# Seven block products for eight in eleven of the gates' and the output product's slots of a decoder block

## The chip, the core and the metric

One core of one Trainium2 chip runs the whole kernel in one launch. TensorE (PE) does the matrix products into eight PSUM banks, ScalarE (ACT) and VectorE (DVE) do the elementwise work, SyncE (SP) issues the DMAs, GpSimd (POOL) does a handful of small operations. The metric is the time of one execution on the device in microseconds (us), the median of several runs.

## The reference, cut to what matters

One layer over 256 tokens of width 2048, all in float32. The lines below are the part that the change touches: two gates, each a product of the normed input with 2048 columns of `w_in`, scale the two branches' up-projections; their sum goes through `w_out`.

```python
h = rmsnorm(x, attn_norm_w[l])
proj = h @ w_in[l]
rq, rk, rv, rg, mq, mk, mv, g_ret, g_moba = jnp.split(proj, split_at, axis=-1)
...
merged = jax.nn.sigmoid(g_ret) * (o_ret @ w_ret_up[l]) + jax.nn.sigmoid(g_moba) * (o_moba @ w_moba_up[l])
x = x + merged @ w_out[l]
h2 = rmsnorm(x, ffn_norm_w[l])
up = causal_dwconv(h2 @ w_ffn_up[l], conv_w[l], conv_b[l])
a, b = jnp.split(up, 2, axis=-1)
x = x + (jax.nn.silu(a) * b) @ w_ffn_down[l]
return rmsnorm(x, final_norm_w)
```

`o_ret` (1024 wide) and `o_moba` (1024 wide) are the results of a chunked retention and of a block attention, which run beside the earlier products.

## The kernel before

**Products.** Each float32 operand is split into two parts, `hi` (a copy rounded to the matmul's type, on ACT) and `lo` (full minus `hi`, on DVE), and a product is the sum of three: hi·hi, hi·lo and lo·hi. `mm3` issues these three matmuls. A matmul of the stretch in question has a stationary block of 128x128 activations and 512 moving columns of weights, and adds into one PSUM bank (128 x 512 float32).

**Slots.** The weights stream in once, as halves of 128x1024 float32 (512 KB: two 128-row pieces of one 512-column group). Two halves make a slot. The loop at L894 runs over the groups of `plan()`: gates `gr` and `gm` (4 slots each, 512 columns per group `c`), up-projections `um` and `ur` (2 slots each), and this for four columns `c`; then `wo` (4 groups of 4 slots), then `up` and the down product `dn`. In a plain slot PE does 2 halves x 2 pieces x 2 token tiles x 3 = 24 matmuls (`products`, L883 to L891).

**What sets the order.** All order is that of the code. While PE works on slot n, the code issues the parts of slot n+1: `part` (L146) puts the `hi` copies on ACT and the `lo` subtractions on DVE, then issues the load for the half four ahead (L144, `RAW_BUFS` is 4, so the raw tile of slot n+1 is that of slot n-1, and it is free when its `lo` is done). `whi` and `wlo` have four buffers (`PART_BUFS`), so the `hi` copies of slot n+1 wait until PE is through with the same half of slot n-1. Elementwise work between the groups is written as generators (`spawn`), of which each runs one stage per slot (`run_tasks`), after that slot's parts; the PE work that they ask for (`flip`, a transpose) goes into the middle of the slot's matmuls (`issue`, L180).

**Names.** `sr` and `sm` hold the gates' sigmoids and then the merged columns (`keep_sig` L470, `gate_moba` L474, `merge` L477); `ftr` are PSUM tiles for the transposes of a merged column into `mgh` and `mgl`, the two parts of `wo`'s activations (`flipped`, L450); `xp` is the residual input that `closed` (L627) adds to `wo`'s result, and `x2` the sum. `acc` is a pair of PSUM banks.

**Seven for eight.** In the down product only, 12 of 44 slots are of another kind: the 2x2 blocks of a slot (two token tiles, two 128-row pieces, two column groups) are multiplied with seven block products in place of eight, so with 21 matmuls. For this `seven_parts` (L674) forms four sums of the weight blocks on DVE (L686 to L691) besides the parts, `seven_sums` (L708) four sums of the activation blocks once per `k`, and the accumulators take eight PSUM banks: four main ones and four extra ones, `e0` to `e3`, which `gathered` (L762) folds into the outputs after the last such slot of a pair of groups.

## Time and profile before

| | us |
|---|---|
| median of 3 runs | 1432.77 (1432.64 to 1432.97) |
| the profiled execution, whole | 1433.07 |
| its span, first to last instruction | 1431.3 |
| PE busy in the span | 1420.4 |
| DVE busy | 977.1 |
| ACT busy | 743.4 |

The table is read from the top: the whole time of the profiled execution is 1.8 us more than its span, and the span is nearly all PE work. The first gate is read out of PSUM (`sr`) at 367 us, and the four `wo` groups are added to the residual from 631 to 699 us; the first matmul on activations' sums, so the first slot of seven products, stands at 1213 us.

### The profile page before, as it was taken

The page shows a single profiled execution, that of the slowest core. Times are in us where ns is not written, and L with a number is a line of the kernel's source. Part 1 is how long each engine was busy: PE and PEld are TensorE (multiplying, and loading weights), DVE is VectorE, ACT ScalarE, POOL GpSimd, SP SyncE. Part 2 cuts the span into 40 slices and gives each one's busy share as a digit, 9 for nine tenths or more (in the row PEclk, how much of TensorE's full clock was granted, in tenths as well). Part 3 has the DMA queues.
Part 4 walks back from the last instruction along what each step waited for, and adds up shares of the span by engine and source line. Part 5 has one row for each costly group of instructions (what it writes and reads, how often), then busy time and mean ns, then how long its engine had stood idle before and what let it go on. Part 6 is the DMA issues. An engine that isn't in the chain of part 4 may idle for free. (4 is left out here: it accounts for less than half of the span.)

```text
span 1431.3 us, 19149 instructions
## 1 busy us (share of the span) xinstructions
PE 1420.4 (99%) x7290; PEld 1214.8 (85%) x7290; DVE 977.1 (68%) x1296; ACT 743.4 (52%) x1006; POOL 6.0 (0%) x14
## 2 busy tenths in 40 slices
PE   9999999999999999999999999999999999999997
PEld 7888888888888888888888888888888888888886
DVE  6687656657554545455567777777777778898787
ACT  6545454544544444444465555555555555555553
POOL 0000000000000000000000000000000000000000
PEclk9999999999999999999999999999999999999999
DMA  8755565555566666666656666565665655656664
GB/s 295 263 181 163 163 190 167 189 175 189 180 186 196 187 195 186 195 214 200 195 188 189 194 182 197 182 195 188 188 194 181 199 181 168 198 192 206 206 215 167
DMA packets 77836, 276.22 MB, mean 193 GB/s; under 512 B 8720, under 2 KB 10288, under 8 KB 77744
## 3 DMA queue, kind: packets, MB, share of 16 engines
q1 hardware_dynamic: 77312, 274.27, 60.3%
q8 instruction: 57, 0.93, 0.3%
q10 hardware_dynamic: 432, 0.73, 0.1%
q14 instruction: 35, 0.29, 0.1%
HBM read 272.86 MB, written 2.10 MB: 192 GB/s over the span
## 5 line engine op out<-in xcount | busy, mean ns | idle before, releaser
L162 DVE TENSOR_TENSOR wlo<-raw,whi 128x1024 fp32r<-128x1024 f32 (+1 forms) x481 | 573.3, 1219 | 373.9 <-ACT whi L161 239.4
L161 ACT ACTIVATE whi<-raw 128x1024 fp32r<-128x1024 f32 (+1 forms) x481 | 502.2, 1056 | 513.7 <-PE acc L170 372.8
L170 PE MATMUL acc<-xb,whi 128*128 128x512 f32 x1920 | 466.2, 392 | 1.2 <-ACT whi L161 1.2
L170 PEld LDWEIGHTS acc<-xb,whi 128*128 128x128 f32 x1920 | 350.7, 188 | 68.8 <-ACT whi L161 2.3
L170 PE MATMUL acc<-whi,xb 128*128 128x512 f32 x896 | 282.1, 391 | 0.0
L170 PEld LDWEIGHTS acc<-xb,wlo 128*128 128x128 f32 x1920 | 250.8, 191 | 12.3
L170 PE MATMUL acc<-xb,wlo 128*128 128x256 f32 x1920 | 254.6, 282 | 0.0
L170 PEld LDWEIGHTS acc<-whi,xb 128*128 128x128 f32 x896 | 168.3, 188 | 34.4
L170 PE MATMUL acc<-wlo,xb 128*128 128x512 f32 x448 | 174.6, 390 | 0.0
L170 PEld LDWEIGHTS acc<-wlo,xb 128*128 128x128 f32 x448 | 84.2, 188 | 16.7
L170 PE MATMUL acc<-wlo,gh 128*128 128x512 f32 x224 | 87.4, 390 | 0.2 <-DVE wlo L162 0.2
L170 PE MATMUL acc<-whi,gl 128*128 128x512 f32 x224 | 87.2, 389 | 0.0
L170 PE MATMUL acc<-whi,gh 128*128 128x512 f32 x224 | 87.1, 389 | 0.0
L521 DVE SCALAR_TENSOR_TENSOR y<-u,vec,y 128x256 f32<-128x256 f32 x176 | 73.5, 480 | 0.0
L170 PEld LDWEIGHTS acc<-wlo,gh 128*128 128x128 f32 x224 | 42.0, 188 | 9.7 <-DVE wlo L162 1.0
L170 PE MATMUL acc<-whi,mgh 128*128 128x512 f32 x128 | 50.1, 392 | 0.0
L170 PE MATMUL acc<-whi,mgl 128*128 128x512 f32 x128 | 49.8, 389 | 0.0
L170 PE MATMUL acc<-wlo,mgh 128*128 128x512 f32 x128 | 49.8, 389 | 0.0
L170 PEld LDWEIGHTS acc<-whi,gh 128*128 128x128 f32 x224 | 42.0, 188 | 8.8
L170 PEld LDWEIGHTS acc<-whi,gl 128*128 128x128 f32 x224 | 42.0, 188 | 8.7
L518 ACT ACTIVATE y<-u,vec 128x256 f32<-128x256 f32 x88 | 47.6, 588 | 0.0
L170 PE MATMUL acc<-whi,otmh 128*128 128x512 f32 x104 | 40.6, 390 | 0.0
(206 smaller groups left out, 1167.9 us busy)
## 6 DMA issues: line engine op xcount, KB each, us to landing
raw<-in_wts SPq DMA_DIRECT2D x503, 512.0 KB, 4.0
rows<-in_x SPq DMA_DIRECT2D x4, 512.0 KB, 6.9
xp<-in_x SPq DMA_DIRECT2D x4, 512.0 KB, 5.2
xt<-in_xT SPq DMA_DIRECT2D x3, 512.0 KB, 7.2
out<-x SPq DMA_DIRECT2D x6, 224.0 KB, 2.9
wf<-in_wf SPq DMA_DIRECT2D x2, 512.0 KB, 7.2
out<-x ACTq DMA_DIRECT2D x2, 352.0 KB, 3.1
xt<-in_xT SPq DMA_DIRECT2D x2, 256.0 KB, 4.5
```

The source lines that it names most:

```text
L161: nc.scalar.activation(hi, full, AF.Copy)
L162: nc.vector.tensor_sub(lo, full, f32(hi))
L170: to.append(lambda: nc.tensor.matmul(out, a, b, **kw))
L518: nc.scalar.activation(y[:, j, :], u[:, j, 0:S], AF.Identity, scale=cv[j][:, 0:1], bias=cv[j][:, 3:4])
L521: nc.vector.scalar_tensor_tensor(y[:, j, :], u[:, j, i:i + S], cv[j][:, i:i + 1], y[:, j, :], op0=OP.mult, op1=OP.add)
```

## The change

The gates, up-projections and output products of the columns after the first leave the general loop and are run by a new function, `middle_slots`, from a list of 52 slots that `middle()` writes. In each of columns 1 to 3 the two gates are now one group of 8 slots, each slot with one half of `gr` and the same half of `gm`; slots 2, 4 and 6 of the 8 are done with seven block products. `um` and `ur` follow, two plain slots each. Groups 0 and 1 of `wo` are paired in the same way, with slots 3 and 5 of 8 in seven products; groups 2 and 3 stay one after the other, four plain slots each. The order of the weights in the stream follows (`order`). The activations' sums are formed in the two slots of the first `ur` (`k` 0 and 1), in slot 4 of column 1 (`k` 2, its `lo` part delayed into the next slot), and for `wo` in the last two slots of column 3.

For the weights' parts a new function, `seven_parts_apart`, is used: it forms three of the four sums in a tile of their own (`tt`), and its parts (`th`, `tl`, 128x1536 each) are the last operations; the raw halves are last read by the two `lo` operations before. The PSUM banks of `acc` and of the four former `att` tiles (`z`) rotate between the roles of main, extra and up-projection banks. The residual input is loaded straight into `x2`, in four DMAs, and the results are added to it in place. The elementwise work on the gates is done in halves of 512 columns: `gates_gathered` folds the four extra banks, `gates_done` adds the main banks and takes the sigmoids.

```diff
+SEVEN_GATES, SEVEN_OUT = (2, 4, 6), (3, 5)
+def paired(first, where, n):
+    rest = list(range(len(where), n))
+    out = []
+    for i in range(n):
+        k = where.index(i) if i in where else rest.pop(0)
+        out.append((i in where, [(g, k) for g in first]))
+    return out
+def middle():
+    out = []
+    for c in range(1, D // CW):
+        out += paired([("gr", c), ("gm", c)], SEVEN_GATES, KD // 2)
+        for g in (("um", c), ("ur", c)):
+            out += [(False, [(g, k), (g, k + 1)]) for k in (0, 2)]
+    out += paired([("wo", 0), ("wo", 1)], SEVEN_OUT, KD // 2)
+    return out + [(False, [(("wo", c), k), (("wo", c), k + 1)]) for c in (2, 3) for k in range(0, KD // 2, 2)]
...
+    at_half, order = {}, []
+    for kind, n, _, _, rows in groups:
+        at_half[kind, n] = sum(r for *_, r in groups[:len(at_half)]) // 256
+    for kind, n, _, _, rows in groups:
+        if kind == "gr" and n == 1:
+            order += [at_half[g] + k for _, two in middle() for g, k in two]
+        if kind == "up" or len(order) < at_half["gr", 1]:
+            order += range(at_half[kind, n], at_half[kind, n] + rows // 256)
+    order += [at_half["dn", c] + k for _, two in down() for k, c in two]
...
+    def seven_parts_apart(n):
+        r, q = raws.pop(n), raws.pop(n + 1)
+        b11, b21, b12, b22 = r[:, :CW], r[:, CW:], q[:, :CW], q[:, CW:]
+        (h1, l1), (h2, l2) = [[wp.tile([P, 2 * CW], F32R, name=x, bufs=PART_BUFS) for x in ("whi", "wlo")]
+                              for _ in range(2)]
+        tt, th, tl = big["tt"], big["th"], big["tl"]
+        nc.vector.tensor_sub(tt[:, 0, :], b12, b11)
+        nc.vector.tensor_sub(b12, b22, b12)
+        nc.vector.tensor_sub(tt[:, 1, :], b22, tt[:, 0, :])
+        nc.vector.tensor_sub(tt[:, 2, :], b21, tt[:, 1, :])
+        while delayed:
+            delayed.pop()()
+        split2(h1, l1, r)
+        split2(h2, l2, q)
+        split2(th, tl, tt)
+        parts[n], parts[n + 1] = (h1, l1), (h2, l2)
+        for i in (0, 1):
+            load(n + i + RAW_BUFS)
...
-    def seven_sums(k):
-
-
-        ah, al = two_blocks(k)
+    def seven_sums(k, pool_k, tag, kind="dn", later=False):
+        ah, al = two_blocks(k, kind)
         room = big["room"]
...
-        pool_k, tag = (px, f"xb{k}") if k < 5 else (big["pf"], "wa")
-        big["s", k] = pool_k.tile([P, 2, 4, P], F32R, name=f"s{k}", tag=tag, bufs=1)
-        split2(big["s", k][:, 0], big["s", k][:, 1], sums)
-
-    def seven_products(k, accs, extra, halves):
-
-        xs = two_blocks(k)
-        sums = big["s", k]
+        big["s", kind, k] = pool_k.tile([P, 2, 4, P], F32R, name=f"s{k}", tag=tag, bufs=1)
+        hi, lo = big["s", kind, k][:, 0], big["s", kind, k][:, 1]
+        nc.scalar.activation(hi, sums, AF.Copy)
+        (delayed.append if later else lambda f: f())(lambda: nc.vector.tensor_sub(lo, sums, f32(hi)))
+    delayed = []
...
+    def gates_gathered(banks_of, sr, sm):
+        e = [banks_of.bank(f"e{i}") for i in range(4)]
+        nc.scalar.activation(sr[:, 0, :], e[0], AF.Copy)
+        nc.vector.tensor_add(sm[:, 0, :], e[2], sr[:, 0, :])
+        nc.vector.tensor_add(sr[:, 1, :], e[3], sm[:, 0, :])
+        nc.vector.tensor_add(sm[:, 1, :], e[1], sr[:, 1, :])
+        nc.vector.tensor_add(sm[:, 0, :], e[1], sm[:, 0, :])
+    def gates_done(banks_of, sr, sm):
+        for j, out in enumerate((sr, sm)):
+            for t in range(NT):
+                nc.vector.tensor_add(out[:, t, :], banks_of.bank((t, j)), out[:, t, :])
+                nc.scalar.activation(out[:, t, :], out[:, t, :], AF.Sigmoid, scale=k1["r1"][:, t:t + 1])
+    def times(two, out):
+        for t in range(NT):
+            nc.vector.tensor_mul(out[:, t, :], two[t], out[:, t, :])
+    def summed_up(two, c):
+        for t in range(NT):
+            x2 = big["x2"][:, t, c * CW:(c + 1) * CW]
+            nc.vector.tensor_add(x2, two[t], x2)
+    def middle_slots(slot, r, free):
+        slots = middle()
+        fa, fb, fc = free
+        t124 = [[big[x][:, i, :] for x in ("th", "tl")] for i in range(3)]
+        sr, sm = now["sr"], now["sm"]
+        for i, (seven, two) in enumerate(slots):
+            c, q = divmod(i, 12)
+            c += 1
+            out = c == D // CW
+            if out or i >= 36:
+                out, q = True, i - 36
+            kind = two[0][0][0]
+            if not out and q == 0:
+                at = Banks([fa, fb], fc + r, [(sv, (0, 1)) for sv, _ in slots[i:i + 8]])
+            elif not out and q in (8, 10):
+                at = Banks([r if q == 8 else fa], [], [(False, (0, 0))] * 2)
+            elif out and q == 0:
+                at = Banks([fa, fb], fc + r, [(sv, (0, 1)) for sv, _ in slots[i:i + 8]])
+            elif out and q in (8, 12):
+                at = Banks([fc if q == 8 else r], [], [(False, (0, 0))] * 4)
+            if out and q == 3:
+                right.close()
+                pr = pool(right, "pr", "right")
+                big["x2"] = pr.tile([P, NT, D], F32, name="x2")
+                for k in ("ss2", "ss3"):
+                    big[k] = sb.tile([P, NT, 4 + (k == "ss3")], F32, name=k)
+            if out and q in (3, 4, 8, 9):
+                w = slice(q // 8 * 2 * CW, (q // 8 + 1) * 2 * CW)
+                nc.sync.dma_start(big["x2"][:, (q - 3) % 5, w], xrows[:, (q - 3) % 5, w])
+            if out and q == SEVEN_OUT[-1] + 2:
+                for _ in gather:
+                    pass
+            elif not out and q == SEVEN_GATES[-1] + 1:
+                gates_gathered(at, sr, sm)
+            n = 2 * (slot + 1)
+            if i + 1 < len(slots) and slots[i + 1][0]:
+                seven_parts_apart(n)
+            else:
+                part(n)
+                part(n + 1)
+            if q == 0:
+                times(r, sr)
+                nc.vector.tensor_add(sr, sr, sm)
+                last_sr = sr
+                if out:
+                    spawn(flips, sr, fc, c - 1, True, after=1)
+                else:
+                    sr = big["pg"].tile([P, NT, CW], F32, name="sr", bufs=2)
+                    sm = big["pg"].tile([P, NT, CW], F32, name="sm", bufs=1)
+            if not out:
+                if c == 1 and q == 4:
+                    seven_sums(2, big["pm"], "s2", "gr", True)
+                if c == D // CW - 1 and q >= 10:
+                    seven_sums(q - 10, big["pm"], f"s{q - 10}", "wo")
+                if q == 8:
+                    gates_done(gates, sr, sm)
+                    spawn(flips, last_sr, fc, c - 1, True)
+                elif q == 10:
+                    times(r, sm)
+                if q == 7:
+                    gates = at
+            else:
+                if q == SEVEN_OUT[-1] + 1:
+                    gather = gathered(at, 0, big["pm"].tile([P, CW], F32, name="v", tag="s2", bufs=1))
+                    next(gather)
+                if q == 8:
+                    for j, bank in enumerate((fa, fb)):
+                        summed_up(bank, j)
+                        spawn(residual, j, bank, after=1 + 2 * j)
+                if q == 12:
+                    summed_up(fc, 2)
+                    spawn(residual, 2, fc, after=1)
+            run_tasks()
+            halves = [parts.pop(2 * slot + h) for h in range(2)]
+            if seven:
+                k = two[0][1]
+                seven_products(two_blocks(k, kind), big["s", "wo" if out else "gr", k], t124, at, halves)
+            else:
+                js = (0, 0) if two[0][0] == two[1][0] else (0, 1)
+                plain_products([(k, j) for (_, k), j in zip(two, js)], lambda k: two_blocks(k, kind), at, halves)
+            issue()
+            slot += 1
+            if not out and q == 11:
+                r, fa, fb, fc = fa, fb, fc, r
+        summed_up(r, 3)
+        spawn(residual, 3, r, after=1)
+        spawn(second_norm, after=1)
+        return slot
...
-        if kind == "dn":
+        if kind == "dn" or kind == "wo" or kind in ("gr", "gm", "um", "ur") and n > 0:
             continue
+        if kind == "up" and n == 0:
+            z = [att("z") for _ in range(4)]
+            slot = middle_slots(slot, two_of(acc), [two_of(last_acc), z[:2], z[2:]])
         nk = rows // P
         act = opened(kind, n)
         two_banks = second_pair if kind == "up" and n % 4 else first_pair
+        last_acc = acc if slot else None
...
+            if kind == "ur":
+                seven_sums(kc, big["pm"], f"s{kc}", "gr")
```

**DVE in column 1 (and 2) of the gates.** The rows below are what stands on VectorE before around a column's end: `wlo<-raw,whi` is a `lo` part of a half, `sm` and `sr` the merging of the gates, `mgl` the `lo` part of a merged and transposed column.

```order
L475 TENSOR_TENSOR sm<-acc,sm 128x1024
L162 TENSOR_TENSOR wlo<-raw,whi 128x1024 x4
L478 TENSOR_TENSOR sr<-acc,sr 128x1024
L479 TENSOR_TENSOR sr<-sr,sm 128x1024
L162 TENSOR_TENSOR wlo<-raw,whi 128x1024 x4
L162 TENSOR_TENSOR mgl<-ftr,mgh 128x512 x2
L162 TENSOR_TENSOR wlo<-raw,whi 128x1024 x16
```

Two slots' `lo` parts (four rows of 1024) stand between the merge and the `mgl` rows, and then 16 with nothing between them: the gates of the next column.

Now, from the merge of column 0 to the parts of slot 4 of column 1 and the sums of `k` 2 (`tt<-raw` and the three rows behind it are the weights' sums, `room` the activations'):

```order
L840 TENSOR_TENSOR sr<-acc,sr 128x512 x2
L890 TENSOR_TENSOR sr<-sr,sm 128x1024
L708 TENSOR_TENSOR tt<-raw 128x512
L709 TENSOR_TENSOR raw<-raw 128x512
L710 TENSOR_TENSOR tt<-raw,tt 128x512
L711 TENSOR_TENSOR tt<-raw,tt 128x512
L187 TENSOR_TENSOR wlo<-raw,whi 128x1024 x2
L187 TENSOR_TENSOR tl<-tt,th 128x1536
L187 TENSOR_TENSOR wlo<-raw,whi 128x1024 x2
L708 TENSOR_TENSOR tt<-raw 128x512
...
L187 TENSOR_TENSOR wlo<-raw,whi 128x1024 x2
L740 TENSOR_TENSOR room<-xb_80 128x512
```

Each of the three marked slots has five rows more than a plain one: four sums and the long `tl` at its end.

**DVE in the output product.** Before, at the start of `wo`: the merge of column 3, two slots' parts, the `mgl` rows of that column.

```order
L478 TENSOR_TENSOR sr<-acc,sr 128x1024
L479 TENSOR_TENSOR sr<-sr,sm 128x1024
L162 TENSOR_TENSOR wlo<-raw,whi 128x1024 x4
L162 TENSOR_TENSOR mgl<-ftr,mgh 128x512 x2
L162 TENSOR_TENSOR wlo<-raw,whi 128x1024 x2
L627 TENSOR_TENSOR x_5238<-acc,xp 128x2x512
```

Now, from the same merge: the parts of `wo`'s slot 2, those of slot 3 (seven products), and only then `mgl`.

```order
L840 TENSOR_TENSOR sr<-z,sr 128x512 x2
L890 TENSOR_TENSOR sr<-sr,sm 128x1024
L187 TENSOR_TENSOR wlo<-raw,whi 128x1024 x2
L708 TENSOR_TENSOR tt<-raw 128x512
L709 TENSOR_TENSOR raw<-raw 128x512
L710 TENSOR_TENSOR tt<-raw,tt 128x512
L711 TENSOR_TENSOR tt<-raw,tt 128x512
L187 TENSOR_TENSOR wlo<-raw,whi 128x1024 x2
L187 TENSOR_TENSOR tl<-tt,th 128x1536
L187 TENSOR_TENSOR mgl<-z,mgh 128x512 x2
```

The reading of the transposes' banks has moved behind the whole of slot 3's parts.

**PE in the gates.** Before, the first half of a plain slot of `gm` (one bank pair, two pieces by two tiles by three matmuls):

```order
L170 MATMUL acc_3857<-whi_3858,xb2_80 128x512
L170 MATMUL acc_3857<-wlo_3859,xb2_80 128x512
L170 MATMUL acc_3857<-whi_3858,xb2_80 128x512 x2
```

Now, the last four of the seven products of slot 2 of column 1, in the order of the code, and the next slot's first matmul (`z` and `acc` are banks, `s0` the activations' sums):

```order
L195 MATMUL acc_3624<-whi_3761,s0_3642 128x512
L195 MATMUL acc_3624<-wlo_3762,s0_3642 128x512
...
L195 MATMUL acc_3624<-th_3622,s0_3642 128x512
L195 MATMUL acc_3624<-tl_3623,s0_3642 128x512
...
L195 MATMUL z_3717<-th_3622,s0_3642 128x512
L195 MATMUL z_3717<-tl_3623,s0_3642 128x512
...
L195 MATMUL acc_3530<-th_3622,xb0_78 128x512
L195 MATMUL acc_3530<-tl_3623,xb0_78 128x512
...
L195 MATMUL acc_3530<-whi_3801,xb5_83 128x512
```

The products that need `th` and `tl` stand last in the slot: twelve matmuls come before them. In the whole program PE now has 5,019 matmuls of 128x512, 5,052 before; all other matmuls and transposes are as many as before.

## Rows read from the trace of the kernel before

**Rows 1.** The page, its parts 1 and 2: the span, the busy time of each engine, and PE's busy share and granted clock in forty slices.

```profile
span 1431.3 us, 19149 instructions
...
PE 1420.4 (99%) x7290; PEld 1214.8 (85%) x7290; DVE 977.1 (68%) x1296; ACT 743.4 (52%) x1006; POOL 6.0 (0%) x14
...
PE   9999999999999999999999999999999999999997
...
PEclk9999999999999999999999999999999999999999
```

**Rows 2.** Who waited for whom, PE and its weight loads (PEld): us in total, times, longest.

```profile
PE idle L647 <- DVE idle L644: 1.2, 1, 1.2
PE acc L170 <- ACT whi L161: 1.2, 1, 1.2
PE acc L170 <- DVE wlo L162: 0.2, 1, 0.2
...
PEld acc L170 <- DVE wlo L162: 1.0, 2, 0.6
PEld acc L170 <- DVE t L695: 0.4, 1, 0.4
```

**Rows 3.** Stretches of the gates (first two) and of the down product (last two): length, busy time of each engine, granted clock, DMA share, GB/s.

```profile
400.00:440.00 40.00, 40.00 (x182) 33.23 (x181) 22.40 (x20) 17.38 (x19) 0.00 (x0) 1.00 0.65 191
440.00:480.00 40.00, 40.00 (x179) 33.10 (x178) 20.18 (x18) 16.95 (x17) 0.00 (x0) 1.00 0.65 193
1212.00:1256.00 44.00, 43.80 (x192) 35.58 (x191) 40.15 (x59) 25.63 (x33) 0.00 (x0) 1.00 0.61 198
1256.00:1300.00 44.00, 44.00 (x195) 36.13 (x194) 39.15 (x54) 24.42 (x29) 0.00 (x0) 1.00 0.63 208
```

**Rows 4.** The timeline of PE and of ACT in a plain slot of `ur` (start, us, what): its first matmul, the first of its second half twelve matmuls later, and the `hi` copy that waits for the half just finished.

```profile
399.09 0.39 PE L170 MATMUL acc<-whi,otrh 128*128 128x512 f32 x1
...
401.81 0.39 PE L170 MATMUL acc<-whi,otrh 128*128 128x512 f32 x1
...
402.06 1.06 ACT L161 ACTIVATE whi<-raw 128x1024 fp32r<-128x1024 f32 x1 [1.66 <-PE acc L170]
```

**Rows 5.** Groups of instructions with their shapes kept apart: count, busy us, mean ns of one, idle before.

```profile
L162 DVE TENSOR_TENSOR wlo<-raw,whi 128x1024 fp32r<-128x1024 f32 x479 | 572.0, 1222 | 373.8 <-ACT whi L161 239.4 <-PE acc L170 81.7 <-issue 52.5
L161 ACT ACTIVATE whi<-raw 128x1024 fp32r<-128x1024 f32 x479 | 501.0, 1058 | 513.7 <-PE acc L170 372.8 <-issue 115.3 <-DMA raw<-in_wts 14.0
...
L687 DVE TENSOR_TENSOR raw<-raw 128x512 f32<-128x512 f32 x12 | 8.3, 692 | 0.4
...
L513 DVE TENSOR_TENSOR y<-acc,y 128x512 f32<-128x512 f32 x44 | 30.1, 684 | 0.0
L512 ACT ACTIVATE y<-acc 128x512 f32<-128x512 f32 x44 | 25.9, 588 | 6.7 <-PE acc L170 6.7
...
L475 DVE TENSOR_TENSOR sm<-acc,sm 128x1024 f32<-128x1024 f32 x4 | 4.9, 1216 | 0.0
...
L161 ACT ACTIVATE s<-room 128x512 fp32r<-128x512 f32 x6 | 3.8, 632 | 20.2 <-DVE room L718 20.2
...
L715 DVE TENSOR_TENSOR room<-room 128x128 f32<-128x128 f32 x6 | 1.8, 292 | 0.2
```

**Rows 6.** The timeline of DVE in the down product, two slots of seven products with one plain slot between them: the end of the first one's parts, the plain slot's two `lo`, the first and the last operation of the second one's parts; and the same activations' sums from first to last.

```profile
1198.33 0.68 DVE L714 TENSOR_TENSOR room<-otrh,otrl 128x512 f32<-128x512 f32 x1
...
1200.77 0.69 DVE L162 TENSOR_TENSOR s<-room,s 128x512 fp32r<-128x512 f32 x1 [0.70 <-ACT s L161]
1201.38 0.42 DVE L162 TENSOR_TENSOR gl<-g,gh 128x256 fp32r<-128x256 f32 x1
...
1349.52 1.22 DVE L695 TENSOR_TENSOR t<-raw,t 128x1024 fp32r<-128x1024 f32 x1
1350.66 2.36 DVE L162 TENSOR_TENSOR wlo<-raw,whi 128x1024 fp32r<-128x1024 f32 x2
1354.39 1.23 DVE L684 TENSOR_TENSOR wlo<-raw,whi 128x1024 fp32r<-128x1024 f32 x1 [1.38 <-ACT whi L682]
...
1360.90 1.23 DVE L695 TENSOR_TENSOR t<-raw,t 128x1024 fp32r<-128x1024 f32 x1
```

**Rows 7.** The timeline of PE for the same two slots: the first matmul of each and its first one on the last parts (`t`).

```profile
1349.29 0.39 PE L170 MATMUL acc<-whi,otrh 128*128 128x512 f32 x1
...
1352.01 1.52 PE L170 MATMUL acc<-t,s 128*128 128x512 f32 x6
...
1359.49 0.39 PE L170 MATMUL acc<-whi,otrh 128*128 128x512 f32 x1
...
1362.21 1.52 PE L170 MATMUL acc<-t,s 128*128 128x512 f32 x6
```

**Rows 8.** The timeline of ACT in the second of these slots: the copies that wait for its two halves to land.

```profile
1353.30 1.06 ACT L682 ACTIVATE whi<-raw 128x1024 fp32r<-128x1024 f32 x1 [1.92 <-DMA raw<-in_wts]
1355.56 0.63 ACT L683 ACTIVATE whi<-raw 128x512 fp32r<-128x512 f32 x1 [1.20 <-DMA raw<-in_wts]
```

**Rows 9.** DMA issues by line: count, KB each, median us from issue to landing. The first two are of the whole span; the third is of the stretch from 400 to 620 us.

```profile
raw<-in_wts SPq DMA_DIRECT2D x503, 512.0 KB, 4.0
...
wf<-in_wf SPq DMA_DIRECT2D x2, 512.0 KB, 7.2
...
raw<-in_wts SPq DMA_DIRECT2D x80, 512.0 KB, 3.6
```

More of the change, by code (lines that the diff above doesn't have):

```diff
@@ L448, in retention, with flips @@
             split2(ot["rh"][:, k, :], ot["rl"][:, k, :], tr[:, i * S:(i + 1) * S], vec[:, V_RET + k:V_RET + k + 1])
-    def flipped(full, dsth, dstl, k0, weight):
-        trs = []
+    def flips(full, two, c, gates):
         for b in range(2):
-            tr = att("ftr")
             for i in range(2):
@@ L741, in seven_products, with plain_products, __init__ @@
             mm3(accs.bank(key), ah, al, bh, bl, begin, end, to=stream)
-    class Banks:
-        def __init__(self, c, main, extra, counts):
-            self.c, self.main, self.extra, self.left = c, main, extra, dict(counts)
-            self.fresh = set(counts)
+    def plain_products(two, xs_of, accs, halves):
+        for (k, j), (hi, lo) in zip(two, halves):
+            xs = xs_of(k)
+            for kk in range(2):
+                w = slice(kk * CW, (kk + 1) * CW)
+                for t in range(NT):
+                    begin, end = accs.edges((t, j), 3)
+                    mm3(accs.bank((t, j)), *(x[:, kk, t * P:(t + 1) * P] for x in xs), hi[:, w], lo[:, w],
+                        begin, end, to=stream)
+    class Banks:
+        def __init__(self, main, extra, slots):
+            self.main, self.extra, self.left = main, extra, {}
+            for seven, two in slots:
+                keys = [(0, 0), (0, 1), (1, 0), "e0", "e1", "e2", "e3"] if seven else [
+                    (t, j) for j in two for t in range(NT) for _ in range(2)]
+                for key in keys:
+                    self.left[key] = self.left.get(key, 0) + 3
+            self.fresh = set(self.left)
         def bank(self, key):
             if isinstance(key, str):
-                i = int(key[1])
-                return self.extra[i // 2][:, i % 2, :]
-            return self.main[key[1]][:, key[0], :]
+                return self.extra[int(key[1])]
+            return self.main[key[1]][key[0]]
         def edges(self, key, n):
@@ L831, in down_slots @@
             if p == 1 and q == per - 2:
-                spawn(added, at.main[0], 2)
+                spawn(added, tiles[1][0], 2)
             run_tasks()
@@ L854, in down_slots @@
             else:
-                for (k, d), (hi, lo) in zip(where, halves):
-                    xs = two_blocks(k)
-                    for j in range(2):
-                        w = slice(j * CW, (j + 1) * CW)
-                        for t in range(NT):
-                            key = (t, d - 2 * p)
-                            begin, end = at.edges(key, 3)
-                            mm3(at.bank(key), *(x[:, j, t * P:(t + 1) * P] for x in xs), hi[:, w], lo[:, w],
-                                begin, end, to=stream)
+                plain_products([(k, d - 2 * p) for k, d in where], two_blocks, at, halves)
                 issue()
```

105 lines of the change are left out of this document (42 added, 63 removed).

## The prediction

> **What bounds the kernel now.** I read the page's first two parts first [rows 1]: PE is busy 1420.4 of 1431.3 us, every slice is full but the last, and the granted clock is full throughout. Then who makes PE wait [rows 2]: outside the start (1.2 us each) it is 0.2 us on PE and 1.4 us on its weight loads, in the whole program. In the gates PE is busy 40.00 of 40.00 us while DVE has 20 to 22 us of work [rows 3]. So PE's matmuls in a row are the time, and everything else is hidden behind them. A matmul taken out is worth its pitch as long as no wait takes its place; the whole question is whether DVE, ACT and the loads still deliver each slot's parts in time.
>
> **What is removed.** A slot's first matmul and the one twelve later start at 399.09 and 401.81 [rows 4]: 2.72 / 12 = 0.2267 us each. A plain slot is 24 x 0.2267 = 5.44 us, a slot of seven products 21 x 0.2267 = 4.76 us. Eleven slots change, each loses three matmuls: 33 x 0.2267 = 7.48 us. The order of the program has just these 33 matmuls fewer and as many transposes, so the change does what it says; that it doesn't is no rival.
>
> **What is added, and its cover.** In a slot of seven DVE does four sums of 512 columns (0.692 each [rows 5], 2.77), two `lo` of 1024 (1.222, 2.44) and one `lo` of 128x1536. No row has that last shape: it lies between a row of 1024 (1.22) and a row of 1024 plus one of 512 (1.22 + 0.68 = 1.91). I take 1.76, the slope of the two added to the first, (1.222 - 0.684) / 512 per column. Together 6.97 us, more than the slot's 4.76; but the neighbour is plain with 2.44. A pair: 9.41 us of DVE on 5.44 + 4.76 = 10.20 us of PE. DVE just keeps up, with 0.79 us to spare per pair, and somewhat more since back to back operations overlap (two `lo` take 2.36, not 2.44 [rows 6]). ACT in a pair: four copies of 1.058 and one of 1536 columns, between 1.06 and 1.69, taken as 1.49 by the same slope: 5.7 us, covered.
>
> The down product shows that this is near the edge. Its seven-slots also come two apart. The first one's last parts end at 1349.52 + 1.22 = 1350.74 and PE takes them at 1352.01, 1.3 us later; the second one's end at 1362.13 and PE takes them at 1362.21 [rows 6, 7]. So the chain there took 1362.13 - 1350.74 = 11.39 us, while PE took 10.20: 1.2 us of lead is lost per repeat, and the gates have three in a row. Why 11.39, with DVE work for some 9.5? The second slot's raw tiles are those of the first, and loads start when its last parts are done: the halves are in use by ACT at 1353.30 and 1355.56 [rows 8], 2.6 and 4.8 us after 1350.74. The changed order frees them earlier: the last readers are the two `lo`, `tl` comes behind. Counted from the end of the first `lo`: 4.82 until both halves are there, 2.77 of sums, 1.22 for the next first `lo` = 8.81 us, under 10.20. So the loads don't set the pace here (they land in 3.6 us in this stretch, 4.0 overall [rows 9]), DVE's 9.41 does, and it gains on PE.
>
> The tight places, one by one. Each seven-slot needs its first `lo` 0.23 us after its start, the `lo` of `th` after 13 matmuls, 2.95 us.
> - Column 1, first: four slots run from the start of the first `ur` slot to it, 4 x 5.44 = 21.76 us, plus 2.95: DVE must be through at 24.7. It can end the first pair of `lo` at 0.25 + 1.06 + 1.22 = 2.5 (ACT starts 0.25 us after PE's half is done [rows 4]); then sums of `k` 0 from 1198.33 to 1201.38 as in the down product, 3.05 with the wait for ACT [rows 6]; `sm` 1.22; two `lo` and the sums of `k` 1, 5.49; two `lo`, two half products and the merge, 2.44 + 1.37 + 1.22; then 6.97. Sum 24.3: 0.4 us in time, without the overlaps.
> - Column 1, third: from there 2.44 + 6.97 + 2.44 + the sums of `k` 2 (0.69 + 4 x 0.29 + 0.69 = 2.5) + 6.97 = 21.3, so 45.6, against 24.7 + 2 x 10.20 = 45.1. Late by 0.5 without overlaps, in time by about 0.5 with a dozen of 0.08 us.
> - Columns 2 and 3 have no sums: from the column's start 2.5 + 1.37 + 1.22 + 6.97 = 12.1 against 2 x 5.44 + 2.95 = 13.8, and 0.79 is gained per pair. No wait.
> - Banks. `um` starts in a bank that `gates_gathered` must have read. Behind the parts of slot 7, which are ready at the latest 0.6 us into that slot, stand four adds (0.684, 2.74) and a `lo` (1.22): 4.6 us, needed at 5.44 + 0.23. No wait; ACT's copy (0.588) lies before it.
> - `wo` slot 3: its first matmul overwrites the bank of the transposes, and `mgl`, which reads it, is queued behind all of that slot's parts. The chain starts when PE leaves slot 1: 0.25 + 1.06 (second `hi`) + 1.49 (`th`) + 1.76 (`tl`) + 0.68 (`mgl`) = 5.24 us of slot 2's 5.44. With the upper ends of the two unknown shapes 5.6, so late by 0.15 at worst; taken as nothing. The `x2` DMAs stand on SP behind the loads of slot 5, which has 0.79 us more lead; nothing.
>
> Everything else that moves (sigmoids, gathering, adding into `x2`) is DVE and ACT work behind plain slots with 5.44 - 2.44 = 3 us to spare each: covered. For the two places of column 1 together I take 0.4 us of wait, between 0 and 1.3.
>
> **The sum.** The profiled execution took 1433.07: 1433.07 - 7.48 + 0.4 = 1426.0. It lay 0.30 above the median of the runs, so on the runs' scale 1432.77 - 7.48 + 0.4 = 1425.7 us.
>
> **Rivals.**
> - The loads set the pace after all, as in the down product: 1.2 us lost per repeat. Column 1 starts with 0.4 of lead: waits of 0.8 and 1.2; columns 2 and 3 start with 1.7: 0.7 each at the third; `wo` has lead enough. 3.4 us: 1428.7. For it: the 11.39 us. Against it: the raw tiles are freed about 3.0 (first) and 1.8 us (second) before the chain's end.
> - The hand-overs of banks and the sums wait more than counted, since each crosses from PE to ACT to DVE and back: two per column and one in `wo`, 0.2 to 0.5 us each, so 1.4 to 3.5 us: 1426.7 to 1428.8. For it: 0.2 us of margin in `wo`, 0.4 in column 1. Against it: in the down product, with DVE at 91% [rows 3], PE waited 1.6 us at most [rows 2].
> - Both together and the first with less lead, 7.5 us: no change, 1432.8.
> - Slower: loads in the gates land as late as the slowest of that size, 7.2 us for the first half [rows 9] and 2.3 more for the second. Then the cycle is 7.2 + 2.3 + 2.77 + 1.22 = 13.5 us, 3.3 over PE's 10.20, in seven repeats (two per column, one in `wo`) 23 us, less some 8 us of lead: 1432.8 - 7.5 + 15 = 1440. It decides from 2.2 us over, so from a second half that lands 8.4 us after its release. For it: only the broadcast loads at the end. Against it: 3.6 us in this stretch at a DMA share of 0.65.
> - Slower by the clock: waits of PE bring its clock to the lower of its two levels (1.2 in place of 2.4 GHz) in the slot after each third seven-slot, 5.44 us more in each of three columns: 1432.8 - 7.5 + 3 x 5.44 + the 3.4 us of waits above = 1445. Nothing in the rows speaks for it: the clock is full in all of them, also in the stretch where PE was 0.2 us short of full.
>
> The Trainium skill, page "TensorE: Matmul & The Clock Gate", section "HAM oscillation — how this bites in real kernels", speaks against short stages between waits: it says that PE, once left without work for long enough, runs what comes next at half its clock, and pays that again each time. The trace here has no such gap between its start and its last slice, so it neither shows nor refutes it; by the rule the last rival would be the outcome, by rows 1 and 3 the first forecast.
>
> **How the numbers follow.** About 0.2% (2.87 us) is what a measurement can tell from no change: 1429.9 to 1435.6 is "same". Forecast 0.68 (1425.7, its own range 1425.0 to 1426.7); loads 0.10; hand-overs 0.13; no change 0.04; slower by loads 0.03, by the clock 0.02. Faster: 0.68 + 0.13 + 0.09 of the 0.10 (a little more than 3.4 us ends in "same") = 0.90; same 0.05; slower 0.05. The range starts at 0.4 us of waits fewer and some of the old 1.6 gone, 1425.0, and reaches over the hand-overs and the loads to 1429.0.
>
> **What would show it.** Right: the matmuls' pitch still 0.227, 33 fewer, the span shorter by about 7, PE waits behind `tl` and `wlo` of column 1 of some tenths and none in columns 2 and 3, DVE busy longer by about 85 us but PE still full in 400 to 700. Wrong: PE waiting for `tl` or `wlo` in every third seven-slot with ACT or DVE waiting for loads before it (the loads); PE waiting for `mgl` or the gathering adds (hand-overs); a granted clock under 1.

## The result, and the profile after

The changed kernel takes 1425.53 us in the median of four runs (1425.29 to 1426.34), the kernel before 1432.87 beside it: a ratio of 0.9950, 95% interval 0.9932 to 0.9967, 7.34 us less. The forecast was 1425.7. Five more runs in a later measurement gave 1425.61 against 1433.11, 7.50 us less. The profiled execution of the changed kernel is its slowest run, 1426.34 with a span of 1424.2. The time outside the span, from the whole time of a run minus its span, differs between the kernels: in the median of the runs it is 1.8 us before and 2.1 us for the changed kernel, and the runs of one kernel agree in it within 0.1 us. So the spans are 7.8 us apart in the later measurement (1431.3 and 1423.5). No profile shows what the extra 0.3 us are.

The page of the changed kernel, busy time and the slices of PE, DVE and the clock, to be held against [rows 1]:

```profile
PE 1413.8 (99%) x7257; PEld 1208.6 (85%) x7257; DVE 1052.5 (74%) x1424; ACT 762.6 (54%) x1026; POOL 6.4 (0%) x14
...
PE   9999999999999999999999999999999999999997
...
DVE  6687656657589878795667777777777778998777
...
PEclk9999999999999999999999999999999999999999
```

The same line of the kernel before:

```profile
DVE  6687656657554545455567777777777778898787
```

DVE has 75.4 us more work, nearly all of it in slices 12 to 18, where it went from about half to 70% busy and more. PE and its clock are full in the same slices.

The waits of PE's weight loads (first five rows), then of PE, in the whole program; in each row the total, the number and the longest, us. Against [rows 2]:

```profile
PEld acc L195 <- DVE t L696: 1.8, 4, 0.6
PEld idle L648 <- DVE idle L645: 1.2, 1, 1.2
PEld acc L195 <- ACT whi L186: 1.1, 2, 0.7
PEld acc L195 <- DVE wlo L187: 1.1, 2, 0.6
PEld acc L195 <- DVE wlo L694: 0.2, 1, 0.2
...
PE idle L648 <- DVE idle L645: 1.2, 1, 1.2
PE acc L195 <- ACT whi L186: 0.5, 1, 0.5
PE acc L195 <- DVE wlo L187: 0.2, 1, 0.2
PE acc L195 <- DVE t L696: 0.2, 1, 0.2
```

None of these comes from the changed stretch. The rows of `idle` and `whi` are the program's start; `t` and `wlo` L694 belong to the down product's old `seven_parts`, whose code was not touched, and `wlo` L187 to its first slots. No row names `tl`, and none lies between 20 and 1190 us.

Busy time by stretch, columns as in [rows 3]:

```profile
400.00:440.00 40.00, 40.00 (x178) 33.10 (x177) 37.32 (x50) 20.31 (x21) 0.00 (x0) 1.00 0.57 183
440.00:480.00 40.00, 40.00 (x182) 33.23 (x181) 30.90 (x35) 19.59 (x24) 0.00 (x0) 1.00 0.68 210
```

In the tightest 40 us DVE is 93% busy (22.40 us before, 37.32 now), and PE is not short of a tenth of a microsecond. The DMA share is 0.57 and 0.68, against 0.65 in both stretches before.

The two shapes that no row of before showed, by the groups with shapes kept apart, 380 to 720 us (count, busy us, mean ns):

```profile
L187 DVE TENSOR_TENSOR tl<-tt,th 128x1536 fp32r<-128x1536 f32 x11 | 19.3, 1752 | 0.2 <-ACT th L186 0.2
...
L186 ACT ACTIVATE th<-tt 128x1536 fp32r<-128x1536 f32 x11 | 16.4, 1491 | 1.9 <-DVE tt L711 1.5
```

1.752 and 1.491 us, against 1.76 and 1.49 estimated.

The leads: the timeline of DVE and then of PE in column 1's first and third seven-slot and in column 2's third. Each pair is the `lo` of the sums' parts and the first matmul that reads it:

```profile
420.44 1.75 DVE L187 TENSOR_TENSOR tl<-tt,th 128x1536 fp32r<-128x1536 f32 x1
441.20 1.75 DVE L187 TENSOR_TENSOR tl<-tt,th 128x1536 fp32r<-128x1536 f32 x1
...
502.07 1.75 DVE L187 TENSOR_TENSOR tl<-tt,th 128x1536 fp32r<-128x1536 f32 x1
```

```profile
423.15 0.39 PE L195 MATMUL acc<-tl,s 128*128 128x512 f32 x1
...
443.56 0.39 PE L195 MATMUL acc<-tl,s 128*128 128x512 f32 x1
...
507.69 0.39 PE L195 MATMUL acc<-tl,s 128*128 128x512 f32 x1
```

Start plus length against PE's start: 422.19 to 423.15 is 0.96 us early, 442.95 to 443.56 is 0.61 early, 503.82 to 507.69 is 3.87 early. The second seven-slots lie at 1.77 (column 1) and 3.07 (column 2), the first of column 2 at 2.26: a gain of 0.8 per pair where no activations' sums stand between.

### The profile page after: what moved, and what is told of

Read it like the earlier page. It is cut to its first block, busy times and chain, and to the rows that moved or that the text cites. A ratio compares the mean times of both kernels' runs of the same rounds, so it can differ in the third digit from the quotient of the medians.

```text
span 1424.2 us, 19249 instructions
## 1 busy us (share of the span) xinstructions
PE 1413.8 (99%) x7257; PEld 1208.6 (85%) x7257; DVE 1052.5 (74%) x1424; ACT 762.6 (54%) x1026; POOL 6.4 (0%) x14
## 5 line engine op out<-in xcount | busy, mean ns | idle before, releaser
L187 DVE TENSOR_TENSOR wlo<-raw,whi 128x1024 fp32r<-128x1024 f32 (+1 forms) x481 | 570.6, 1219 | 285.1 <-ACT whi L186 150.2
L195 PE MATMUL acc<-whi,xb 128*128 128x512 f32 x610 | 195.4, 391 | 0.0
L195 PEld LDWEIGHTS acc<-whi,xb 128*128 128x128 f32 x610 | 114.6, 188 | 23.5
L195 PE MATMUL acc<-wlo,xb 128*128 128x512 f32 x305 | 118.9, 390 | 0.0
L195 PEld LDWEIGHTS acc<-wlo,xb 128*128 128x128 f32 x305 | 57.3, 188 | 11.1
L195 PE MATMUL z<-whi,xb 128*128 128x512 f32 x178 | 58.0, 389 | 0.0
L195 PEld LDWEIGHTS z<-whi,xb 128*128 128x128 f32 x178 | 33.4, 188 | 6.9
L195 PE MATMUL z<-wlo,xb 128*128 128x512 f32 x89 | 34.6, 389 | 0.0
L195 PE MATMUL acc<-whi,otmh 128*128 128x512 f32 x88 | 34.5, 392 | 0.0
```

The costliest lines, as they stand in the source:

```text
L187: nc.vector.tensor_sub(lo, full, f32(hi))
L195: to.append(lambda: nc.tensor.matmul(out, a, b, **kw))
```

## The experiments

All ran in turn with the kernel before on the same chip, in five rounds or more. The dose in column 2, the long dose and the plain output product ran on the chip of the changed kernel's second measurement and are held against its 1425.61, the others against 1425.53.

The traces say where each kernel gains or loses. PE's matmuls are the same in all kernels up to the first `ur` slot of column 0 and from the first matmul of `up` on (the last kernels below differ in the down product too), so three starts of matmuls cut the program into a start, a middle that holds the change, and a rest with `up` and the down product. The first matmul of that `ur` slot in the changed kernel (before: 399.09 [rows 4]), and the last one of `wo`, first before, then changed:

```profile
398.45 0.39 PE L195 MATMUL acc<-whi,otrh 128*128 128x512 f32 x1
```

```profile
698.91 0.39 PE L170 MATMUL acc<-whi,mgl 128*128 128x512 f32 x1
```

```profile
690.79 0.39 PE L195 MATMUL z<-whi,mgl 128*128 128x512 f32 x1
```

The same two starts, and that of the program's last matmul, from PE's timeline of every profile, in us. The rest runs from the last matmul of `wo` to the program's last; the last column is the whole time minus the span in the median of the runs.

| profile | the start ends at | middle | rest | outside the span |
|---|---|---|---|---|
| before | 399.09 | 299.82 | 723.70 | 1.8 |
| changed | 398.45 | 292.34 | 724.77 | 2.1 |
| changed, once more | 398.49 | 292.34 | 724.19 | 2.1 |
| no seven products | 399.29 | 299.83 | 723.93 | 1.8 |
| output product plain | 398.74 | 293.70 | 725.17 | 1.8 |
| old order of the parts | 398.73 | 296.86 | 723.68 | 1.8 |
| dose in column 1 | 398.70 | 293.95 | 723.68 | 2.1 |
| dose in column 2 | 398.40 | 292.35 | 723.64 | 2.1 |
| long dose in column 1 | 398.70 | 302.31 | 723.67 | 2.1 |
| new order in the down product | 398.56 | 292.35 | 723.47 | 1.9 |
| the same, once more | 398.90 | 292.34 | 723.47 | 1.9 |
| thirteen slots of seven | 398.36 | 292.38 | 722.78 | 1.7 |

Each row is one execution. The changed kernel's middle comes out alike within 0.04 us in the five profiles that have it unaltered, so larger differences of the middle are the kernel's. The start and the rest also move from one execution to the next; the rest's part ahead of the down product's first seven-slot is 513.5 us in every profile, so what moves there is the down product.

**Only the new order, no seven products.**

```diff
-SEVEN_GATES, SEVEN_OUT = (2, 4, 6), (3, 5)
+SEVEN_GATES, SEVEN_OUT = (), ()
```

(with the sums and the folding of the extra banks taken out)

> The changed kernel with its new order of slots, but with 24 matmuls in every slot from the first gate column to the output product: no sums of blocks, no folding of extra banks. Theory (only the count of matmuls matters, all else is hidden): 33 x 0.2267 = 7.48 us more than the changed kernel, so 1433.0 within 0.4, level with the kernel before. Rival (the reorganisation itself, residual straight into x2 and gates in pairs, gives or costs time): it differs from the kernel before by more than 0.7 us, one way or the other.

Measured: 1432.95, the kernel before 1432.94 beside it, ratio 1.0000 (0.9991 to 1.0008). The pairing of the gates, the rotation of banks and the residual straight into `x2` are worth nothing either way that shows: the middle takes 299.83 us, 299.82 before. The changed kernel's middle is 7.48 us shorter than both, to the hundredth what 33 matmuls are by the pitch (7.42 us in the medians). So the 33 matmuls are the whole gain, and the added work costs nothing.

**The output product's two made plain.**

```diff
-SEVEN_GATES, SEVEN_OUT = (2, 4, 6), (3, 5)
+SEVEN_GATES, SEVEN_OUT = (2, 4, 6), ()
```

(with their sums and their folding taken out)

> The changed kernel with the two seven-slots of the output product made plain again (no sums of the merged activations' blocks, no folding there), the nine of the gates as they are. Theory (every seven-slot pays its three matmuls): 6 x 0.2267 = 1.36 us more, 1426.9 within 0.4. Rival (the output product's two pay nothing, since their hand-overs of banks eat it): within 0.4 us of the changed kernel.

Measured: 1427.08, 1.47 us over the changed kernel on the same chip, in runs from 1426.54 to 1428.09; the middle is 1.36 us longer, six matmuls. The theory held: these two slots pay in full, though their hand-over has the least margin of all (below).

**The old order of the parts in the middle.** `seven_parts`, which sums in the raw tiles and reads them last, in place of `seven_parts_apart`:

```diff
-                seven_parts_apart(n)
+                seven_parts(n)
```

(with `seven_parts` fitted to the middle's tiles)

> The changed kernel with the weights' parts in the middle formed in the order of the old down product: three of the sums in the raw tiles, whose last readers are then the last operations. Theory (the refill sets the pace in that order, some 1.2 us of lead lost per pair of slots where the new order gains 0.8): leads of 0.96, 1.77, 0.61 us in column 1 and 2.25, 2.7 to 3.1, 3.5 to 3.9 in columns 2 and 3 become about 1, -0.2, -1.4 and 2.2, 1.0, -0.2; PE waits 1.2 to 1.6 us in column 1 and 0 to 0.5 in each of the others: 1.2 to 2.6 us more than the changed kernel, 1426.7 to 1428.1. Rival (DVE's busy time sets the pace and the order of its operations does not matter): within 0.4 us of the changed kernel and no wait of PE between 380 and 640 us.

Measured: 1429.48 (ratio to before 0.9977, 0.9968 to 0.9986), 3.95 us over the changed kernel, more than expected. PE's waits in the stretches 440 to 480 us (the first three rows) and 600 to 720 us (the last):

```profile
PE acc L195 <- DVE wlo L699: 0.9, 1, 0.9
PE acc L195 <- ACT whi L694: 0.4, 1, 0.4
PE z L195 <- DVE tl L701: 0.2, 1, 0.2
...
PE z L195 <- DVE mgl L187: 1.7, 1, 1.7
```

The middle is 4.52 us longer than the changed kernel's; in the medians 0.3 us less outside the span stand against it, and waits in the down product that differ from one execution to the next. Column 1 is near what was expected, 1.5 us of waits on PE (its weight loads show 2.6), and by the starts of its matmuls PE loses 2.3 us there; columns 2 and 3 show no wait on PE and 0.2 on its weight loads. Another 2.0 us are a wait that the expectation did not have, and no load is part of it: in `wo` the copy L689, ahead of the sums in this order, waits for PE, and the `lo` of the last merged column, `mgl`, stands behind the chain that follows, so PE waits for the bank that it reads.

```profile
616.48 0.63 ACT L689 ACTIVATE whi<-raw 128x512 fp32r<-128x512 f32 x1 [2.56 <-PE acc L195]
```

Where the chain of column 1 lost its time, from ACT's and DVE's timelines of this kernel: the copies that wait for the load, and the last parts of column 1's first two seven-slots:

```profile
425.25 1.06 ACT L688 ACTIVATE whi<-raw 128x1024 fp32r<-128x1024 f32 x1 [1.86 <-DMA raw<-in_wts]
427.38 0.63 ACT L689 ACTIVATE whi<-raw 128x512 fp32r<-128x512 f32 x1 [1.07 <-DMA raw<-in_wts]
```

```profile
421.53 1.23 DVE L701 TENSOR_TENSOR tl<-raw,th 128x1024 fp32r<-128x1024 f32 x1
...
432.73 1.22 DVE L701 TENSOR_TENSOR tl<-raw,th 128x1024 fp32r<-128x1024 f32 x1
```

The raw tiles are released at 422.76, ACT has the two halves 2.5 and 4.6 us later, and the next chain ends 11.2 us after the first, where PE takes 10.20. DVE stands idle for 1.80 us in that pair, for these two copies. In the changed kernel the same two ends lie 9.4 us apart, and there too DVE waits for a load, but less. Its rows in the same pair: the two `lo` that read the raw tiles last, the next slot's first sum, and that slot's `tl`; then the first sum of column 3's second seven-slot, the longest of these waits:

```profile
418.18 2.36 DVE L187 TENSOR_TENSOR wlo<-raw,whi 128x1024 fp32r<-128x1024 f32 x2
...
424.91 0.69 DVE L708 TENSOR_TENSOR tt<-raw 128x512 f32<-128x512 f32 x1 [0.44 <-DMA raw<-in_wts]
...
429.84 1.75 DVE L187 TENSOR_TENSOR tl<-tt,th 128x1536 fp32r<-128x1536 f32 x1
...
552.21 0.69 DVE L708 TENSOR_TENSOR tt<-raw 128x512 f32<-128x512 f32 x1 [0.76 <-DMA raw<-in_wts]
```

The raw tiles are free at 420.54, the second half is there 4.4 us later, and four sums and two `lo` take the 5.0 us to the next release: 9.4 us. So the refill sets the pace of this pair in both orders. What the new order changes is how much stands in its round: 11.2 us in the old one, above PE's 10.20, and 9.4 in the new one, below it.

**A dose of work on DVE, in column 1 and in column 2.** Three idle subtractions of 512 columns ahead of the parts of the third seven-slot (for column 2 the same with `c == 2`):

```diff
+            if not out and c == 1 and q == 5:
+                for _ in range(3):
+                    nc.vector.tensor_sub(big["dose"], f32(big["th"][:, 0, :]), f32(big["th"][:, 1, :]))
```

> The changed kernel with three idle subtractions of 512 columns on VectorE (3 x 0.69 = 2.1 us) ahead of the parts of column 1's third seven-slot, where the last part is 0.61 us early. Theory (VectorE's chain decides there and the lead is what the trace shows): PE waits 2.1 - 0.61 = 1.5 us for tl, once; 1427.0 within 0.4. Rival (the chain has slack elsewhere, for example VectorE itself waiting for loads or copies in that stretch): less than 0.5 us. Rival (the delay runs on into the bank that um takes over): over 2 us.

> The changed kernel with the same three idle subtractions on VectorE (2.1 us) at the same place of column 2, ahead of the parts of its third seven-slot, where the last part is 3.87 us early. Theory (the leads read from the trace of the changed kernel are what counts, and column 2 has gained 0.8 per pair): the dose is hidden, within 0.4 us of the changed kernel, no wait of PE between 480 and 520 us, and the lead falls to about 1.8 us. Rival (what the dose in column 1 cost is a price of VectorE's work anywhere in these slots): again 1.3 us more, 1426.9.

Measured: 1426.86 in column 1, 1.33 us over the changed kernel; 1425.36 in column 2, level with it (1425.61). The matmul of column 1 that waits, with the length and what it waited for:

```profile
442.50 0.50 PE L195 MATMUL z<-wlo,xb 128*128 128x512 f32 x1 [1.25 <-DVE wlo L187]
```

It is the slot's first `lo`, not `tl` as the expectation said: in the changed kernel the first `lo` is needed 2.7 us before `tl` (440.83 against 443.56) and is done 2.8 us before it (438.93 + 1.22 against 441.20 + 1.75), so the two have nearly the same lead, and the earlier one meets the wait. The two `lo` in the changed kernel's timeline:

```profile
438.93 2.35 DVE L187 TENSOR_TENSOR wlo<-raw,whi 128x1024 fp32r<-128x1024 f32 x2
```

The same 2.1 us on the same engine cost nothing in column 2, where the trace had 3.87 us of lead; 1.93 are left in that kernel's own trace (503.96 + 1.75 against 507.64). The middle says the same, 1.61 us longer with the dose in column 1 and 0.01 with that in column 2. So the lead read off the two timelines tells how long a delay a place bears.

**The dose in column 1 four times as long** (`range(12)`).

> The changed kernel with twelve idle subtractions (12 x 0.69 = 8.3 us) at the place of the first dose, ahead of the parts of column 1's third seven-slot. Three of them made PE wait 1.2 to 1.7 us and cost 1.3 us, so 0.6 us of 2.1 were hidden. Theory (a wait costs its length and nothing behind it): 8.3 - 0.7 = 7.6 us more than the changed kernel, 1433.1 within 0.6, the granted clock full behind the wait. Rival (the clock falls to its lower level after such a wait): the clock shows under 1 behind 445 us, and the time is higher by up to one slot's worth, 7.6 + 5.4 = 13.0 us more, 1438.5.

Measured: 1435.50, 9.9 us over the changed kernel, between the two theories. Stretches of 4 us of this kernel (columns as in [rows 3]), then PE's timeline behind the wait:

```profile
440.00:444.00 4.00, 1.25 (x6) 0.71 (x4) 3.79 (x7) 0.00 (x0) 0.00 (x0) 1.00 0.00 0
444.00:448.00 4.00, 0.00 (x0) 0.00 (x0) 3.93 (x7) 1.83 (x2) 0.00 (x0) 0.80 0.00 0
448.00:452.00 4.00, 3.10 (x7) 2.48 (x8) 4.00 (x4) 3.09 (x4) 0.00 (x0) 0.50 0.54 152
452.00:456.00 4.00, 4.00 (x16) 3.24 (x15) 3.31 (x4) 2.12 (x2) 0.00 (x0) 0.84 0.78 237
456.00:460.00 4.00, 4.00 (x19) 3.30 (x19) 3.95 (x5) 1.06 (x1) 0.00 (x0) 1.00 0.52 155
```

```profile
448.90 0.80 PE L195 MATMUL z<-wlo,xb 128*128 128x512 f32 x1 [7.65 <-DVE wlo L187]
449.50 0.63 PE L195 MATMUL z<-whi,xb 128*128 128x512 f32 x1
449.92 0.63 PE L195 MATMUL acc<-whi,xb 128*128 128x512 f32 x1
450.35 0.63 PE L195 MATMUL acc<-wlo,xb 128*128 128x512 f32 x1
...
453.31 0.40 PE L195 MATMUL acc<-whi,s 128*128 128x512 f32 x1
453.54 0.39 PE L195 MATMUL acc<-th,s 128*128 128x512 f32 x1
```

PE waits 7.65 us; meanwhile the granted clock falls to 0.50, the lower of its two levels (1.2 in place of 2.4 GHz), and stays there behind the wait. Eleven matmuls, from 448.90 to 453.54, take 4.64 us in place of 11 x 0.2267 = 2.49, so 2.1 us more: 7.65 + 2.1 = 9.8 of the measured 9.9. The rule cited ahead of the result (the Trainium skill, page "TensorE: Matmul & The Clock Gate", section "HAM oscillation — how this bites in real kernels") agrees with this one wait; whether the price is paid again at each of several waits was not tried. The Trainium skill, page "TensorE: Matmul & The Clock Gate", section "Wait — 56ns, not 53.3ns?", gives 426.7 ns from start to start for 512 columns at the lower level, and the three rows from 449.50 on start 0.42 and 0.43 us apart. Around the wait of 1.25 us in the short dose and that of 1.7 us in the old order the granted clock is 1.00 in each 4 us stretch. They cost PE some 0.3 us more than their rows say (1.61 and 2.0 us), in part since a row counts from the end of the matmul before, which the profile puts 0.39 us behind its start, while the pitch is 0.2267.

**The changed kernel once more.**

> The changed kernel unaltered, on the chip of these runs, to have its waits of the down product a second time. Theory (the 2.0 us of waits for t in the down product belong to that one execution, which lay 0.8 us over the median): 1425.5 within 0.3, with fewer waits for t, 0.4 to 1.2 us. Rival (they belong to the kernel): again 1.8 to 2.2 us.

Measured: 1425.61, and waits for `t` of 1.1 us in its profile (three of them, on the weight loads), against 1.8 in the profile above and 0.4 in the one of before. They move from one execution to the next, and the rest with them: 724.77 us in the profile with 1.8, 724.19 with 1.1, 723.64 to 723.68 in the three profiles of the doses, which have 0.4. The theory held.

**The new order in the down product.** Sums in tiles of their own there too, for 11 of its 12 seven-slots (the first keeps the old one, since the `u` and `y` tiles that hold the sums are still in use):

```diff
+    def seven_parts_down(n):
...
+        nc.vector.tensor_sub(t14[:, :CW], b12, b11)
+        nc.vector.tensor_sub(b12, b22, b12)
+        nc.vector.tensor_sub(t2, b22, t14[:, :CW])
+        nc.vector.tensor_sub(t14[:, CW:], b21, t2)
+        split2(h1, l1, r)
+        split2(h2, l2, q)
+        split2(big["t2"][:, 0, :], big["t2"][:, 1, :], t2)
+        split2(*big["t14"], t14)
```

> The changed kernel with the order of the new function in 11 of the 12 seven-slots of the down product too (sums in tiles of their own, raw tiles free before the last parts). Theory (PE's waits for t and wlo in the down product, 2.0 us in the profile of the changed kernel, come from raw tiles that are freed late): those waits go, 0.5 to 2 us less, 1423.5 to 1425.0; the 1.2 us around 1150 to 1200 us, ahead of the down product, stay. Rival (they come from VectorE being full, 91% busy there, and the order does not matter): within 0.4 us of the changed kernel, the waits for t remain.

> The kernel with the new order of parts in the down product, unaltered, on the chip of this run. Theory (its gain over the changed kernel holds and is not one chip's): 1425.0 within 0.3, no wait for t. Rival: level with the changed kernel, 1425.5 to 1425.6.

Measured: 1424.98 and, on another chip, 1425.11, each with a ratio to before of 0.9945 (0.9932 to 0.9957): 7.96 and 7.86 us under the kernel before beside it, where the changed kernel lay 7.34 and 7.50 under it. So the gain is about 0.5 us in the medians, at the lower edge of what was expected, and 0.2 of it lie outside the span (1.9 us against 2.1); the intervals of the ratios overlap, and it is the profiles that speak for it. The waits of PE's weight loads in its profile, whole program:

```profile
PEld acc L195 <- ACT whi L186: 2.2, 3, 1.2
...
PEld acc L195 <- DVE wlo L187: 1.1, 2, 0.7
```

The waits for `t` are gone. What stays of `wlo` lies in the down product's first slots, between 1206 and 1250 us, not ahead of it as the expectation had it. The rest takes 723.47 us in both profiles of this order. Against that, the two profiles of the changed kernel and those of the doses lose 1.3, 0.7 and 0.2 us there, where the rows of their weight loads add up to 2.0 (`t` and `wlo` L694), 1.1 and 0.4. So a weight load's wait is only partly PE's, and what the new order is worth depends on how much an execution with the old one waits.

**One more slot of seven, in the down product's second half.**

```diff
-SEVEN = ((4, 7, 10, 13, 16, 18), (3, 5, 8, 10, 13, 15))
+SEVEN = ((4, 7, 10, 13, 16, 18), (3, 5, 7, 9, 11, 13, 15))
...
+            if p == 1 and q == 12:
+                seven_sums(6, None, 7)
```

> The kernel with the new order of parts in the down product, and in its second half a seventh slot of seven products (slots 3, 5, 7, 9, 11, 13, 15 of 22), whose activations' sums are formed once more on VectorE late in that half and lie over activations that are used up. Theory (with the raw tiles free early VectorE gains on PE by 10.2 - 9.6 = 0.6 us per pair, so the half has room for another slot and its 2.5 us of sums): 3 x 0.2267 = 0.68 us less than with twelve, 1424.3 within 0.3. Rival (the second half has no lead to give: seven in a row at every other slot make PE wait): as with twelve or slower, and waits for t or wlo between 1330 and 1400 us.

Measured: 1424.23 (ratio to before 0.9939, 0.9926 to 0.9953), 0.88 under the same kernel with twelve (1425.11 on the same chip); expected 0.68. The rest is 0.69 us shorter, the three matmuls; the other 0.2 lie outside the span (1.7 us against 1.9). In the stretch that is dense now, 1330 to 1400 us (columns as in [rows 3]):

```profile
1330.00:1400.00 70.00, 70.00 (x310) 57.90 (x309) 60.77 (x71) 36.09 (x39) 0.00 (x0) 1.00 0.67 214
```

DVE is 87% busy and PE full, with no wait for `t`. This version beats both kernels: 8.7 us under the one before beside it, and some 1.3 under the changed one. Whether the old order would have had room for the thirteenth slot was not tried.

## Why the prediction was right

- **The matmuls removed, 7.48 us.** Right, and the whole of it: 7290 - 7257 = 33 fewer on PE, the pitch is still 0.227 (442.42 to 443.56 in five of them), the middle is 7.48 us shorter, and the same order without the seven products is level with before.
- **The unknown prices.** 1.76 and 1.49 us were measured as 1.752 and 1.491: the slope between two known shapes carried half as far again. DVE's added work was put at 85 us and is 75.4.
- **The refill.** The step that the changed order frees the raw tiles early enough was the one that decided, and it held: 9.4 us per pair, under PE's 10.20. Its working did not. It counted 8.81 us for the round of the loads and 9.41 for DVE's work, and took DVE to set the pace. DVE's work takes 9.39 - 0.44 = 8.95 us back to back, and the round of the loads takes the 9.39: the working began it at the end of the first `lo`, but the second half is released only by the second one, and both are there 5.5 us after the first in place of 4.82. That 9.41 was said and 9.4 came is luck. With the old order the cycle is 11.2 us and the kernel 3.95 slower; the rival's price was 3.4. But of the two rivals it took both parts: column 1 as the loads rival said, hardly anything in columns 2 and 3 (0.7 each was counted), and a hand-over in `wo`, where it had said there was lead enough.
- **The wait of 0.4 us in column 1.** This step failed: no such wait is there. The first seven-slot was to be 0.4 us early and is 0.96; the third was put between 0.5 late and 0.5 early and is 0.61 early. The sum of single durations was 0.5 to 1.1 us too long, since operations back to back overlap; the working named these overlaps and then took a wait all the same. Without it the forecast would have been 1425.3; the measured medians lie between the two. That the forecast came within 0.2 us of them is in part luck: in place of the 0.4 that did not come stand amounts that the sum did not have, 0.3 us more outside the span, and in the two profiles 0.6 us less at the start and 1.1 and 0.5 more in the down product.
- **Columns 2 and 3.** 1.7 us of lead at the first and 0.79 more per pair were counted; column 2 shows 2.26, 3.07, 3.87. Column 3 gains less, 2.25, 2.73, 3.48: there DVE waits 0.76 and 0.42 us for the loads.
- **The hand-overs.** In `wo` a margin of 0.2 us was counted. DVE's first `mgl` ends near 618.6 (the row below holds two of equal length) and PE takes the bank at 618.97:

```profile
617.93 1.28 DVE L187 TENSOR_TENSOR mgl<-z,mgh 128x512 fp32r<-128x512 f32 x2
```

```profile
618.97 0.39 PE L195 MATMUL z<-whi,mgh 128*128 128x512 f32 x1
```

So it holds by some 0.3 us, and the old order, 1.7 to 2.2 us late there, shows what it was worth.
- **The clock.** The rival's price was wrong: it put 5.44 us on each time that the clock falls, for a whole slot at the lower level. The long dose, the one wait of that kind here, shows 2.1 us. Its condition, waits long enough to bring the clock down, never came near: the kernel has no wait at all in that stretch.
- **Not looked at.** The down product was taken as unchanged. Its waits for `t` differ between executions of one kernel by more than the 0.4 us that the forecast argued over.

## What to carry to other kernels

When one engine is full, the worth of a change is its work taken out times its pitch, and the question is only the lead of what feeds it: read, slot by slot, the end of the last part against its first use, and count by the pair of slots whether that lead grows or shrinks. Where a buffer's last reader is also the last step of a chain, the refill is added to every repeat; moving results into tiles of their own, so that the buffer is freed in the middle of the chain, turned 11.2 us per pair into 9.4 here; in the down product that order has room for another slot. A wait named on a weight load is only in part time lost: 2.0, 1.1 and 0.4 us of such rows went with 1.3, 0.7 and 0.2 us. To tell effects of this size apart, compare stretches between the same matmuls: they repeat within 0.04 us here, while the medians also hold the start, other stages and the time outside the span.

## What the runs showed of the hardware that was not expected

The granted clock fell during a wait of 7.65 us, and was full again after ten matmuls at the lower level, 2.1 us dearer in all; two single waits of 1.25 and 1.7 us left it at 1.00. The loads of weights landed later in the denser stretch, by the issues from 400 to 620 us of the changed kernel (count, KB each, median us to landing), against 3.6 before [rows 9]:

```profile
raw<-in_wts SPq DMA_DIRECT2D x81, 512.0 KB, 4.2
```

DVE waits 0.4 to 0.8 us for such a load in four of the six pairs of the gates, PE for none; why they land later with nearly as many in the same time was not tried.
